# Rows of the modulation product in buffers of their own beside the branch merge, and another order of the first norm

## Chip, cores, metric

The kernel runs on one core of a Trainium2 chip. The metric is the device time of one execution in microseconds. Three runs are shown, and their median counts.

## What is computed

The reference is one layer of a diffusion backbone over 512 latent tokens of width 1024 and 256 context tokens. Cut to the parts that the change touches:

```python
mx = (sil_c @ w_ada[l] + b_ada[l])[:, None, :]          # modulation: 6 vectors of 1024
xsh1, xsc1, xg1, xsh2, xsc2, xg2 = jnp.split(mx, N_ADA, axis=-1)
px = _split_in(_modulate(x, xsh1, xsc1) @ w_in[l])
...
mix_x = _merge(px['merge_gate'], hgrn_out, conv_out, ox_att @ w_att_o[l], w_out[l])
x = _layer_norm(ALPHA * x + xg1 * mix_x, ln1_g[l], ln1_b[l])
x = _layer_norm(ALPHA * x + xg2 * _peer(_modulate(x, xsh2, xsc2), peer_wq[l], ...), ...)
```

`_merge` is the sum over three branches of sigmoid(gate) times the branch's output product, then a product with `w_out`. `_peer` makes queries (16 products with `wq`), picks the 16 best experts of each head and token, and evaluates gelu of tokens times all rows of `peer_u` (128 products here, called u products) for three of the four token blocks, with gathers for block 0.

## The kernel before

Data lie transposed, features on the 128 partitions. A float32 product is done in three passes (`mm3`): each operand is split into a high part (rounded copy, ScalarE, `whi`) and a low part (difference, VectorE or GpSimd, `wlo`), and TensorE adds low*high, high*low and high*high. A weight of 128 output columns is 512 KB; `wload` fetches it on SP's queue into one of 3 buffers `wraw`, splits it in two halves into 8 buffers each of `whi` and `wlo` (four weights), and a product over it is 24 matmuls. The orders of TensorE, VectorE, ScalarE and GpSimd are written out by hand: what stands in the code first is issued first. SP's order is left to the framework.

Weights come through a list: `want` appends, `fetch_next(n)` loads and splits the next one if fewer than n (3) stand ready, `feed` hands over the next one and fetches it on the spot if none is ready. `go` takes one step of a generator, `run` all of it.

**The merge.** After the 8 products of the HGRN branch (`hg`, evacuated by the multiply in line 749) a loop over 8 column blocks does two products each: the gate (`'in', Z_MG + KT + j`; sigmoid in line 781 into `s`) and the convolution branch (`'conv', j`; multiply in line 788, then GpSimd's add in line 789). Each loop turn also does four of the 32 rows of the modulation vectors that are needed later (`adas`): a row of `w_adaT` (512 KB) times silu(c), summed over the free axis by one VectorE instruction (line 763, shown as CUSTOM_DVE). The rows pass through the same list and the same 3 `wraw` buffers as the weights:

```python
for n, w in ((0, ('in', Z_MG + KT + j)), (2, ('conv', j)), (3, None)):
    want(*[('ada', a) for a in steps[:n] if a is not None])
...
if w[0] == 'ada':
    raw = wp.tile([128, KT, 128], F32, name="wraw", bufs=3)
    nc.sync.dma_start(raw, src)
```

So each turn has six items in a list that is at most three ahead, with four calls of `fetch_next`. The attention follows the merge; its first products wait for the last multiply of the merge, since the PSUM pool changes there.

**Norm 1.** After attention and the output projection (`project(h_, b)`, half h_ of block b, blocks in the order 1, 2, 3, 0) each block gets its residual and statistics on VectorE (`project`, `moments1`), the scale by a power on GpSimd (`pspow`, line 154) and a GpSimd multiply (line 1149), the normalisation on ScalarE (`normalise`, line 1154), transposes on TensorE (`turn1`), modulation out of PSUM (`modulate`, half on VectorE in line 1177, half on ScalarE in line 1175) and the split into `thl` (`parts1`). The u product 0 needs blocks 1 to 3 and fills the time while block 0 is finished (tile `pu`); the first query product needs all blocks. After that the expert search (top-k) runs on VectorE beside the query and u products.

Of the kernel before, what the change touches and what calls it, by code (L numbers as in the profile page):

```python
# [94 lines left out]
def body(tc, I, O):  # L95
# [139 lines left out]
    TABLE = {'hg': 'w_hg_o', 'conv': 'w_conv_o', 'att': 'w_att_o'}  # L235
    LOWS = {'in': (V, G), 'hg': (V, G), 'conv': (V, G), 'att': (V, V)}

    def source(kind, *i):
        if kind == 'ada':
            return I['w_adaT'][i[0]].rearrange("p (k e) -> p k e", e=128), None  # L240
        if kind == 'u':
            return I['uT'][i[0]].rearrange("p (k e) -> p k e", e=128), (V, G)
        return I[TABLE.get(kind, 'w_in')][i[0]], LOWS[kind]

# [17 lines left out]
    def fetch_next(n=3):  # L262

        if todo and len(ready) < n:
            w = todo.pop(0)
            src, subs = source(*w)
            if w[0] == 'ada':
                raw = wp.tile([128, KT, 128], F32, name="wraw", bufs=3)
                nc.sync.dma_start(raw, src)
                ready.append((w, raw))  # L270
                return
            ready.append((w, wload(None, subs, loaded.pop(0)) if loaded else wload(src, subs)))
# [17 lines left out]
    want(*[('hg', j) for j in range(KT)])  # L290
    steps = [a for j in range(32) for a in ((j,) if j % 4 < 3 else (j, None))]
    for j in range(KT):
        for n, w in ((0, ('in', Z_MG + KT + j)), (2, ('conv', j)), (3, None)):
            want(*[('ada', a) for a in steps[:n] if a is not None])
            del steps[:n]
            want(*([w] if w else []))
    want(*[('in', z) for z in (Z_AK, Z_AQ, Z_AV, Z_AQ + 1)])
# [461 lines left out]
    def adas():  # L759

        for j in range(32):
            raw = feed('ada', j)[:].rearrange("p k e -> p (k e)")
            V.tensor_tensor_reduce(out=raw, in0=raw, in1=silb, scale=1.0, scalar=0.0, op0=ALU.mult, op1=ALU.add,
                                   accum_out=mod[:, 16 + j, 0:1])
            yield
            if j % 4 == 3:
                m = mod[:, 13 + j:17 + j, 0]
                V.tensor_add(m, m, bada[:, 13 + j:17 + j])
                yield
# [80 lines left out]
    want(*[('in', Z_MG + 16 + j) for j in range(KT)])  # L850
    want(*[('att', j) for j in range(KT)], ('u', 0))

# [250 lines left out]
    pus = ExitStack()  # L1103
    pu = pus.enter_context(tc.tile_pool(name="pu", bufs=1, space=PSUM))
    ops = ExitStack()
# [24 lines left out]
    def project(h_, b):  # L1130
# [5 lines left out]
        sl = slice(h_ * 512, h_ * 512 + 512)  # L1136
        V.tensor_mul(t_, ps, g1[:, sl])
        V.scalar_tensor_tensor(x1[:, b, sl], x1[:, b, sl], ALPHA, t_, op0=ALU.mult, op1=ALU.add)
        V.bn_stats(bst[b][:, h_, :], x1[:, b, sl])
# [3 lines left out]
    def moments1(b):  # L1143
# [4 lines left out]
        pspow(rs[:, 0:1], mv[:, 1:2], 1.0, mv[:, 1:2])  # L1148
        G.tensor_mul(rs[:, 1:2], rs[:, 0:1], mv[:, 0:1])

    def normalise(b):
        xb = x1[:, b, :]
        rs = moms[b]
        A.activation(xb, xb, AF.Identity, scale=rs[:, 0:1], bias=rs[:, 1:2])
        nc.scalar.dma_start(x1d[b], xb)

# [11 lines left out]
    def modulate(b, pts):  # L1168
        tfs = []
        for q_, pt in enumerate(pts):  # L1170
            tf = op.tile([128, 4, 128], F32, name="tf", bufs=4)
            for i in range(4):
                j = q_ * 4 + i
                if q_ or b == 3:
                    A.activation(tf[:, i, :], pt[:, i, :], AF.Identity, scale=gs[:, j:j + 1], bias=bs[:, j:j + 1])
# [5 lines left out]
    def parts1(b, tfs):  # L1181
        for q_, tf in enumerate(tfs):
            sl = (slice(None), slice(q_ * 4, q_ * 4 + 4), slice(b * 128, b * 128 + 128))
            split(thl[0][sl], thl[1][sl], tf)

# [8 lines left out]
    for i, b in enumerate(BLOCKS):  # L1194
        wout(4 + i)
        project(0, b)
    thl = [xp.tile([128, KT, T], F32R, name=n) for n in ("xh", "xl")]
    for i, b in enumerate(BLOCKS[:3]):
        project(1, b)
        if i:  # L1200
# [7 lines left out]
        fetch_next(4)  # L1208
    project(1, 0)
    pts = turn1(3)  # L1210
    moments1(0)
    tfs = modulate(3, pts)
    fetch_next(4)
    parts1(3, tfs)
    normalise(0)
    for _ in range(3):
# [3 lines left out]
    ttok = x1p.tile([128, D], F32, name="ttok")  # L1220
    us = pu.tile([128, T], F32, name="pu")[:, :T - 128]
    p_ = product(us, feed('u', 0), [t_[:, :, 128:] for t_ in thl], 4)
    go(p_)
    pts = turn1(0)
    go(p_)
    tfs = modulate(0, pts)
    parts1(0, tfs)
    UV = {}
    UV['q', 0] = wload(I['wq'][0], (V, G))
    fetch_next(4)  # L1230
    turn_back(tfs)
# [23 lines left out]
    arun = gap.tile([128, NA, TD], F32, name="gt")  # L1255
    A.activation(arun[:, 0, :], us, AF.Gelu_apprx_tanh)
    pus.close()
# [39 lines left out]
    for h in range(H):  # L1297
        u0 = 1 + sum(AHEAD[:h])
        items += [('q', 2 * h), ('q', 2 * h + 1)] + [('u', u0 + i) for i in range(AHEAD[h])]
    items += [('u', i) for i in range(1 + sum(AHEAD), NU)]  # L1300
    SUBS = {'q': (G, G), 'u': (G, G)}
# [493 lines left out]
```

## Time and profile before

| | |
|---|---|
| median of 3 runs | 2467.76 us (2458.68 to 2470.45) |
| the profiled execution | 2469.7 us, span 2467.8 us |
| TensorE busy | 2356.6 us (95%), granted clock 0.986 of full speed on average |
| VectorE busy | 1937.8 us (79%) |
| ScalarE, GpSimd busy | 1044.3 us (42%), 667.5 us (27%) |
| DMA | 452.66 MB, mean 183 GB/s |

The span is the stretch between the first and the last instruction in the trace; times below are microseconds from its start. Busy shares are means over stages with different limits, so each stage is read by itself. Matmuls are pipelined, so a busy TensorE is not one at its peak.

### The profile page before, as it was taken

How to read it: one execution, taken by the hardware profiler on the slowest of the kernel's cores; microseconds unless marked ns; L12 is line 12 of the kernel's file. 1: busy time of each engine (PE TensorE's matmuls, PEld its weight loads, DVE VectorE, ACT ScalarE, POOL GpSimd, SP SyncE). 2: the span in 40 equal slices, each digit the busy share in tenths (PEclk: the TensorE clock that was granted, in tenths of full speed). 3: DMA queues.
4: the chain of work that ended last, by engine and by line, in shares of the span. 5: the costliest groups of instructions: out<-in, count | busy, mean ns of one | idle time of the engine just before them, and what ended most of it. 6: DMA issues, size and time to landing. Idle time of an engine off the chain costs nothing.

```text
span 2467.8 us, 34756 instructions
## 1 busy us (share of the span) xinstructions
PE 2356.6 (95%) x12547; PEld 2028.7 (82%) x12547; DVE 1937.8 (79%) x3722; ACT 1044.3 (42%) x2298; POOL 667.5 (27%) x564
## 2 busy tenths in 40 slices
PE   7999999999988999999999999999999999999997
PEld 3888888887767777787899999987777889898886
DVE  7788888887665566564899789968878888889886
ACT  5544444434312444643457655533333333333333
POOL 6000000003122000031688401122323344444432
PEclk9999999999999999999999999999999999999999
DMA  6211111112364111132333368999999989999962
GB/s 243 69 60 61 61 60 60 52 65 72 134 212 158 43 35 35 52 111 103 105 112 103 121 241 308 330 321 317 335 368 348 350 317 344 324 336 320 331 223 96
DMA packets 156973, 452.66 MB, mean 183 GB/s; under 512 B 16256, under 2 KB 60672, under 8 KB 154624
## 3 DMA queue, kind: packets, MB, share of 16 engines
q1 hardware_dynamic: 106976, 278.33, 32.7%
q0 software_dynamic: 36864, 134.23, 15.3%
q10 hardware_dynamic: 12960, 37.87, 4.1%
q8 instruction: 99, 1.62, 0.3%
q14 instruction: 74, 0.61, 0.1%
HBM read 411.77 MB, written 37.03 MB: 182 GB/s over the span
## 4 chain that ended last, share of the span: by engine, by line
PE 57%; DVE 25%; DMA 6%; ACT 5%; issue 4%; POOL 2%; ACTq 0%; DVEq 0%; SPq 0%; POOLq 0%
PE mm L142 13%; PE mm L144 12%; PE mm L143 12%; DVE wlo L131 6%; DVE raw L1488 3%; DVE ttok L1496 3%; DMA wraw<-in_v_dram 3%; ACT whi L129 2%; PE sc L466 2%; PE pg L1538 2%; ACT ph L137 2%; DMA wraw<-in_uT_dram 2%; PE acc L142 1%; PE acc L143 1%; PE acc L144 1%
## 5 line engine op out<-in xcount | busy, mean ns | idle before, releaser
L131 DVE TENSOR_TENSOR wlo<-wraw,whi 128x512 fp32r<-128x512 f32 x680 | 453.1, 708 | 186.1 <-ACT whi L129 184.2
L142 PE MATMUL mm<-xh,wlo 128*128 128x512 f32 (+1 forms) x1456 | 559.7, 384 | 17.8 <-DVE wlo L131 5.5
L143 PE MATMUL mm<-xl,whi 128*128 128x512 f32 (+1 forms) x1456 | 540.3, 371 | 1.1 <-POOL xl L327 0.9
L144 PE MATMUL mm<-xh,whi 128*128 128x512 f32 (+1 forms) x1456 | 540.5, 371 | 0.0
L129 ACT ACTIVATE whi<-wraw 128x512 fp32r<-128x512 f32 x784 | 447.5, 621 | 121.3 <-DMA wraw<-in_w_in_dram 46.2
L142 PE MATMUL acc<-whi,pl 128*128 128x512 f32 x756 | 300.4, 397 | 23.9 <-DVE pl L138 18.8
L142 PEld LDWEIGHTS mm<-xh,wlo 128*128 128x128 f32 x1456 | 275.8, 189 | 53.1 <-DVE wlo L131 6.8
L144 PEld LDWEIGHTS mm<-xh,whi 128*128 128x128 f32 x1456 | 275.0, 189 | 37.2
L143 PEld LDWEIGHTS mm<-xl,whi 128*128 128x128 f32 x1456 | 275.8, 189 | 34.0 <-DVE xl L327 1.8
L143 PE MATMUL acc<-wlo,ph 128*128 128x512 f32 x756 | 301.5, 399 | 2.1 <-DVE wlo L131 0.9
L144 PE MATMUL acc<-whi,ph 128*128 128x512 f32 x756 | 298.6, 395 | 0.0
L1477 POOL DMA_INDIRECT raw<-in_u_dram,idx x128 | 147.4, 1151 | 472.1 <-DVE act L1488 413.5
L1477 POOL DMA_INDIRECT raw<-in_v_dram,idx x128 | 160.5, 1254 | 193.0 <-DVE ttok L1496 156.1
L142 PEld LDWEIGHTS acc<-whi,pl 128*128 128x128 f32 x756 | 143.8, 190 | 62.4 <-ACT whi L129 16.7
L137 ACT ACTIVATE ph<-a 128x384 fp32r<-128x384 f32 x94 | 49.4, 525 | 332.5 <-DVE a L1601 323.3
L561 DVE SCALAR_TENSOR_TENSOR u<-up,dw,u 128x512 f32<-128x512 f32 x240 | 179.6, 748 | 4.9
L131 POOL TENSOR_TENSOR wlo<-wraw,whi 128x512 fp32r<-128x512 f32 x104 | 149.2, 1457 | 123.0 <-ACT whi L129 116.6
L143 PEld LDWEIGHTS acc<-wlo,ph 128*128 128x128 f32 x756 | 143.7, 190 | 42.7 <-DVE wlo L131 13.4
L144 PEld LDWEIGHTS acc<-whi,ph 128*128 128x128 f32 x756 | 143.6, 190 | 28.5
L1496 DVE SCALAR_TENSOR_TENSOR ttok<-raw,act,ttok 128x1024 f32<-128x1024 f32 x127 | 162.9, 1283 | 3.1
L142 PE MATMUL pa<-xh,wlo 128*128 128x384 f32 x456 | 154.7, 339 | 6.4 <-DVE wlo L131 6.4
L144 PE MATMUL pa<-xh,whi 128*128 128x384 f32 x456 | 154.5, 339 | 0.0
(422 smaller groups left out, 4255.6 us busy)
## 6 DMA issues: line engine op xcount, KB each, us to landing
wraw<-in_uT_dram SPq DMA_DIRECT2D x128, 512.0 KB, 5.0
wraw<-in_v_dram SPq DMA_DIRECT2D x128, 512.0 KB, 6.2
wraw<-in_w_in_dram SPq DMA_DIRECT2D x96, 512.0 KB, 3.3
gd<-gs ACTq DMA_DIRECT2D x16, 1536.0 KB, 7.5
gr<-gd SPq DMA_DIRECT2D x60, 288.0 KB, 9.1
wraw<-in_w_adaT_dram SPq DMA_DIRECT2D x32, 512.0 KB, 4.4
wraw<-in_wq_dram SPq DMA_DIRECT2D x16, 512.0 KB, 3.3
ad<-a ACTq DMA_DIRECT2D x39, 192.0 KB, 4.2
```

The lines of the kernel that those rows point to most:

```text
L129: A.activation(hi, r, AF.Copy)
L131: subs[i].tensor_sub(lo, r, hi.bitcast(F32))
L137: A.activation(hi, src, AF.Copy)
L142: P.matmul(out, ll, rh, start=first, stop=False)
L143: P.matmul(out, lh, rl, start=False, stop=False)
L144: P.matmul(out, lh, rh, start=False, stop=last)
L466: P.matmul(x_.ps[:, b, :], x_.KM[:, b * 128:(b + 1) * 128], ap3(x_.QP, T + b * 128, [2 * w_, 64 // w_], [w_ - T, 2], [1, w_]), start=True, ...
L561: V.scalar_tensor_tensor(acc, up[:, i:i + T], dw[:, j, i:i + 1], acc, op0=ALU.mult, op1=ALU.add)
L1477: G.indirect_dma_start(out=r, out_offset=None, in_=I['u'] if n < NS_ else I['v'], in_offset=bass.IndirectOffsetOnAxis(ap=idx0[:, n % NS_:n ...
L1488: V.tensor_tensor_reduce(out=r, in0=r, in1=ttok, scale=1.0, scalar=0.0, op0=ALU.mult, op1=ALU.add, accum_out=act[:, s_:s_ + 1])
L1496: V.scalar_tensor_tensor(ysb, r, act[:, s_:s_ + 1], ysb, op0=ALU.mult, op1=ALU.add)
L1538: P.matmul(ps[:, i, :], o3[:, q_, :, i], o1[:, i, :], start=q_ == 0, stop=q_ == 1)
```

## The change

The rows of `w_adaT` leave the list. They get a tile of their own of four rows, in the place of the tile `ohi` (the high part of the HGRN output, free after the last `hg` product), loaded three rows ahead of the reduction. The low parts of the conv weights are made on VectorE alone. In norm 1, the last projection (block 0) only evacuates PSUM before block 3 is modulated and split; its residual and statistics come behind that. The multiply behind the power moves from GpSimd to VectorE, the write of the normalised block to DRAM moves behind the split, block 0 is normalised in two halves, VectorE takes five of eight modulations of block 3, and GpSimd makes the low parts of block 2. Two u products instead of one are computed ahead of the queries (`PRE = 2`), so the later u products are one fewer; the gelu of both stands before the queries' evacuation.

```diff
-    LOWS = {'in': (V, G), 'hg': (V, G), 'conv': (V, G), 'att': (V, V)}
+    LOWS = {'in': (V, G), 'hg': (V, G), 'conv': (V, V), 'att': (V, V)}
...
-            if w[0] == 'ada':
-                raw = wp.tile([128, KT, 128], F32, name="wraw", bufs=3)
-                nc.sync.dma_start(raw, src)
-                ready.append((w, raw))
-                return
...
-    steps = [a for j in range(32) for a in ((j,) if j % 4 < 3 else (j, None))]
     for j in range(KT):
-        for n, w in ((0, ('in', Z_MG + KT + j)), (2, ('conv', j)), (3, None)):
-            want(*[('ada', a) for a in steps[:n] if a is not None])
-            del steps[:n]
-            want(*([w] if w else []))
+        want(('in', Z_MG + KT + j), ('conv', j))
...
     def adas():
-        for j in range(32):
-            raw = feed('ada', j)[:].rearrange("p k e -> p (k e)")
+        raws = mp.tile([128, 4, D], F32, name="ohi")
+        for j in range(-3, 32):
+            if j + 3 < 32:
+                nc.sync.dma_start(raws[:, (j + 3) % 4, :], I['w_adaT'][j + 3])
+            if j < 0:
+                continue
+            raw = raws[:, j % 4, :]
             V.tensor_tensor_reduce(out=raw, in0=raw, in1=silb, scale=1.0, scalar=0.0, op0=ALU.mult, op1=ALU.add,
                                    accum_out=mod[:, 16 + j, 0:1])
...
-    pu = pus.enter_context(tc.tile_pool(name="pu", bufs=1, space=PSUM))
+    PRE = 2
+    pu = pus.enter_context(tc.tile_pool(name="pu", bufs=PRE, space=PSUM))
...
         V.tensor_mul(t_, ps, g1[:, sl])
+        yield
         V.scalar_tensor_tensor(x1[:, b, sl], x1[:, b, sl], ALPHA, t_, op0=ALU.mult, op1=ALU.add)
...
-        G.tensor_mul(rs[:, 1:2], rs[:, 0:1], mv[:, 0:1])
+        V.tensor_mul(rs[:, 1:2], rs[:, 0:1], mv[:, 0:1])
...
-        A.activation(xb, xb, AF.Identity, scale=rs[:, 0:1], bias=rs[:, 1:2])
-        nc.scalar.dma_start(x1d[b], xb)
+        for xb in ([x1[:, b, :]] if b else [x1[:, b, :512], x1[:, b, 512:]]):
+            A.activation(xb, xb, AF.Identity, scale=rs[:, 0:1], bias=rs[:, 1:2])
...
-                if q_ or b == 3:
+                if j > 4 if b == 3 else q_:
...
-            split(thl[0][sl], thl[1][sl], tf)
+            A.activation(thl[0][sl], tf, AF.Copy)
+            (G if b == 2 else V).tensor_sub(thl[1][sl], tf, thl[0][sl].bitcast(F32))
+        nc.scalar.dma_start(x1d[b], x1[:, b, :])
...
-    project(1, 0)
+    last = project(1, 0)
+    go(last)
     pts = turn1(3)
-    moments1(0)
     tfs = modulate(3, pts)
     fetch_next(4)
     parts1(3, tfs)
+    run(last)
+    moments1(0)
     normalise(0)
...
-    us = pu.tile([128, T], F32, name="pu")[:, :T - 128]
-    p_ = product(us, feed('u', 0), [t_[:, :, 128:] for t_ in thl], 4)
+    us = [pu.tile([128, T], F32, name="pu")[:, :T - 128] for _ in range(PRE)]
+    p_ = chain([product(us[i], feed('u', i), [t_[:, :, 128:] for t_ in thl], 4) for i in range(PRE)])
+    go(p_)
+    fetch_next(4)
     go(p_)
     pts = turn1(0)
-    go(p_)
     tfs = modulate(0, pts)
-    parts1(0, tfs)
     UV = {}
     UV['q', 0] = wload(I['wq'][0], (V, G))
-    fetch_next(4)
+    parts1(0, tfs)
+    run(p_)
     turn_back(tfs)
```

Three places show how the instructions move. First ScalarE in the merge, between two sigmoids of gate products (`mm_6038` is the product of gate j = 1; the weight split from `wraw_6072` is the conv weight of j = 1, the product right behind that gate, and `wraw_6113` is the gate weight of j = 2, the next one). Before:

```order
L781 ACTIVATE ms_6069<-mm_6038 128x512
L129 ACTIVATE whi_6074<-wraw_6072 128x512
L129 ACTIVATE whi_6078<-wraw_6072 128x512
L129 ACTIVATE whi_6115<-wraw_6113 128x512
L129 ACTIVATE whi_6119<-wraw_6113 128x512
L781 ACTIVATE ms_6156<-mm_6125 128x512
```

The same place of the change (`mm_6058` is again gate j = 1; `wraw_6114` and `wraw_6154` are the gate and conv weights of j = 3, four and five products further on):

```order
L775 ACTIVATE ms_6097<-mm_6058 128x512
L129 ACTIVATE whi_6116<-wraw_6114 128x512
L129 ACTIVATE whi_6120<-wraw_6114 128x512
L129 ACTIVATE whi_6156<-wraw_6154 128x512
L129 ACTIVATE whi_6160<-wraw_6154 128x512
L775 ACTIVATE ms_6180<-mm_6141 128x512
```

The splits behind a sigmoid are now those of weights that TensorE reads one pair of products or more later, not of the next product.

Second, SP's queue in the merge before (`in_w_in` are gate weights, `in_w_conv_o` conv weights, `in_w_adaT` modulation rows):

```order
L124 DMA wraw<-in_w_conv_o_dram 128x1024
L269 DMA wraw<-in_w_adaT_dram 128x1024 x2
L124 DMA wraw<-in_w_in_dram 128x1024
L269 DMA wraw<-in_w_adaT_dram 128x1024 x2
L124 DMA wraw<-in_w_conv_o_dram 128x1024
```

and of the change, from the first load of a modulation row on:

```order
L124 DMA wraw<-in_w_conv_o_dram 128x1024
L753 DMA ohi<-in_w_adaT_dram 128x1024 x8
L124 DMA wraw<-in_w_in_dram 128x1024
L753 DMA ohi<-in_w_adaT_dram 128x1024 x3
L124 DMA wraw<-in_w_conv_o_dram 128x1024
L753 DMA ohi<-in_w_adaT_dram 128x1024
L124 DMA wraw<-in_w_in_dram 128x1024
```

Before, rows and weights take turns in one ring of three buffers. Now six weights of the merge stand ahead of the first row, and rows go to another tile.

Third, VectorE at the end of norm 1 before (`tf<-pt` is a modulation, `xl<-tf` the low part, `t<-mm` the evacuation of the last projection, BN_STATS and BN_AGGR its statistics):

```order
L1137 TENSOR_TENSOR t<-mm,g_9579 128x512
L1138 SCALAR_TENSOR_TENSOR x_9571<-x_9571,t 128x512
L1139 BN_STATS bst_9608<-x_9571 128x6
L1145 BN_AGGR bmv<-bst_9608 128x2
L1146 TENSOR_SCALAR bmv<-bmv 128x1
L153 TENSOR_SCALAR bmv<-bmv 128x1
L138 TENSOR_TENSOR xl<-tf,xh 128x4x128 x2
L1177 TENSOR_SCALAR tf<-pt,gs,bs 128x128 x4
L138 TENSOR_TENSOR xl<-tf,xh 128x4x128 x2
L131 TENSOR_TENSOR wlo<-wraw,whi 128x512 x2
```

and in the change:

```order
L1132 TENSOR_TENSOR t<-mm,g_9558 128x512
L1172 TENSOR_SCALAR tf<-pt,gs,bs 128x128 x5
L1180 TENSOR_TENSOR xl<-tf,xh 128x4x128 x2
L1134 SCALAR_TENSOR_TENSOR x_9550<-x_9550,t 128x512
L1135 BN_STATS bst_9587<-x_9550 128x6
L1141 BN_AGGR bmv<-bst_9587 128x2
L1142 TENSOR_SCALAR bmv<-bmv 128x1
L153 TENSOR_SCALAR bmv<-bmv 128x1
L1145 TENSOR_TENSOR brs<-brs,bmv 128x1
L1172 TENSOR_SCALAR tf<-pt,gs,bs 128x128 x4
L131 TENSOR_TENSOR wlo<-wraw,whi 128x512
L1180 TENSOR_TENSOR xl<-tf,xh 128x4x128 x2
```

Block 3 now comes ahead of the statistics of block 0, and the first query weight's low part ahead of the low parts of block 0. On TensorE the 8 transposes of block 0 stood behind 12 matmuls of the u product; they now stand behind 36.

## Rows read from the trace of the kernel before

**Rows 1.** The page: shares of the last-ending chain, and the low-part group's row.

```profile
PE 57%; DVE 25%; DMA 6%; ACT 5%; issue 4%; POOL 2%; ACTq 0%; DVEq 0%; SPq 0%; POOLq 0%
L131 DVE TENSOR_TENSOR wlo<-wraw,whi 128x512 fp32r<-128x512 f32 x680 | 453.1, 708 | 186.1 <-ACT whi L129 184.2
```

**Rows 2.** Windows in the merge: length, five engines' busy time, clock, DMA share, GB/s.

```profile
655.00:770.00 115.00, 97.08 (x383) 75.20 (x381) 72.47 (x105) 21.24 (x38) 30.87 (x14) 0.94 0.63 213
660.00:670.00 10.00, 10.00 (x44) 7.86 (x43) 6.92 (x11) 1.75 (x3) 2.21 (x1) 1.00 0.82 274
770.00:780.00 10.00, 8.62 (x36) 7.14 (x37) 4.05 (x8) 3.37 (x6) 1.29 (x1) 0.83 0.58 194
```

**Rows 3.** Timeline of VectorE before and in the merge (start, us, instruction, idle before).

```profile
649.10 0.69 DVE L749 TENSOR_TENSOR mix<-mm,mix 128x512 f32<-128x512 f32 x1 [3.54 <-PE mm L144]
654.70 0.69 DVE L749 TENSOR_TENSOR mix<-mm,mix 128x512 f32<-128x512 f32 x1 [4.91 <-PE mm L144]
666.15 0.68 DVE L788 TENSOR_TENSOR ms<-mm,ms 128x512 f32<-128x512 f32 x1
...
681.43 1.21 DVE L763 CUSTOM_DVE_ANT_0 wraw<-wraw,silb 128x1024 f32<-128x1024 f32 x1
...
682.57 2.31 DVE L763 CUSTOM_DVE_ANT_0 wraw<-wraw,silb 128x1024 f32<-128x1024 f32 x1
...
770.65 0.68 DVE L788 TENSOR_TENSOR ms<-mm,ms 128x512 f32<-128x512 f32 x1
```

**Rows 4.** Timelines of ScalarE and TensorE: one turn of the merge, and its end.

```profile
701.18 0.60 ACT L781 ACTIVATE ms<-mm 128x512 f32<-128x512 f32 x1 [6.10 <-PE mm L144]
701.67 1.14 ACT L129 ACTIVATE whi<-wraw 128x512 fp32r<-128x512 f32 x2
708.88 1.15 ACT L129 ACTIVATE whi<-wraw 128x512 fp32r<-128x512 f32 x2 [6.07 <-DMA wraw<-in_w_in_dram]
...
703.07 0.50 PE L142 MATMUL mm<-uhi,wlo 128*128 128x512 f32 x1 [1.99 <-DVE wlo L131]
...
771.38 0.50 PE L142 MATMUL mm<-xh,wlo 128*128 128x512 f32 x1 [2.75 <-DVE ms L788]
```

**Rows 5.** The tile wraw from 655 to 770: its 47 loads, issue to landing.

```profile
DMA to landing us min/median/max: 3.1/4.3/5.5
```

**Rows 6.** Timelines of TensorE, ScalarE and VectorE at norm 1.

```profile
1167.01 0.44 PE L142 MATMUL pu<-xh,wlo 128*128 128x384 f32 x1 [3.34 <-ACT xh L137]
...
1170.66 1.73 PE L1164 MATMUL pt<-ident,x 128*128 128x128 f32 x8
...
1172.58 0.33 PE L144 MATMUL pu<-xh,whi 128*128 128x384 f32 x1
...
1174.14 0.34 PE L144 MATMUL pu<-xh,whi 128*128 128x384 f32 x1
...
1176.44 0.50 PE L142 MATMUL mm<-xh,wlo 128*128 128x512 f32 x1 [1.09 <-DVE wlo L131]
...
1163.55 2.88 ACT L1175 ACTIVATE tf<-pt,bs,gs 128x128 f32<-128x128 f32 x8
...
1168.39 1.24 ACT L1154 ACTIVATE x<-x,brs 128x1024 f32<-128x1024 f32 x1 [0.92 <-POOL brs L1149]
...
1173.82 1.16 ACT L137 ACTIVATE xh<-tf 128x512 fp32r<-128x512 f32 x2
...
1159.76 1.36 DVE L1177 TENSOR_SCALAR tf<-pt,gs,bs 128x128 f32<-128x128 f32 x4
...
1188.63 0.89 DVE L1372 MAX8 vv<-sk 128x8 f32<-128x128 f32 x4 [3.55 <-PE sk L1331]
```

**Rows 7.** Windows of the later stages: top-k, gate products, gathers (columns as above).

```profile
1260.00:1280.00 20.00, 20.00 (x106) 18.09 (x105) 19.90 (x97) 12.51 (x65) 17.11 (x18) 1.00 0.35 111
...
1520.00:1540.00 20.00, 20.00 (x165) 19.21 (x164) 19.83 (x29) 11.28 (x16) 2.29 (x2) 1.00 0.94 332
...
1760.00:1800.00 40.00, 37.41 (x159) 29.28 (x158) 31.06 (x56) 14.32 (x27) 10.71 (x10) 1.00 1.01 376
```

More of the change, by code (lines that the diff above doesn't have):

```diff
@@ L235, in body @@
     TABLE = {'hg': 'w_hg_o', 'conv': 'w_conv_o', 'att': 'w_att_o'}
-    LOWS = {'in': (V, G), 'hg': (V, G), 'conv': (V, G), 'att': (V, V)}
+    LOWS = {'in': (V, G), 'hg': (V, G), 'conv': (V, V), 'att': (V, V)}
     def source(kind, *i):
-        if kind == 'ada':
-            return I['w_adaT'][i[0]].rearrange("p (k e) -> p k e", e=128), None
         if kind == 'u':
@@ L850, in body @@
     want(*[('in', Z_MG + 16 + j) for j in range(KT)])
-    want(*[('att', j) for j in range(KT)], ('u', 0))
+    want(*[('att', j) for j in range(KT)], ('u', 0), ('u', 1))
     kTs, Vas = {}, {}
@@ L1148, in moments1 @@
         pspow(rs[:, 0:1], mv[:, 1:2], 1.0, mv[:, 1:2])
-        G.tensor_mul(rs[:, 1:2], rs[:, 0:1], mv[:, 0:1])
+        V.tensor_mul(rs[:, 1:2], rs[:, 0:1], mv[:, 0:1])
     def normalise(b):
-        xb = x1[:, b, :]
         rs = moms[b]
-        A.activation(xb, xb, AF.Identity, scale=rs[:, 0:1], bias=rs[:, 1:2])
-        nc.scalar.dma_start(x1d[b], xb)
+        for xb in ([x1[:, b, :]] if b else [x1[:, b, :512], x1[:, b, 512:]]):
+            A.activation(xb, xb, AF.Identity, scale=rs[:, 0:1], bias=rs[:, 1:2])
     def turn1(b):
@@ L1195, in body @@
         wout(4 + i)
-        project(0, b)
+        run(project(0, b))
     thl = [xp.tile([128, KT, T], F32R, name=n) for n in ("xh", "xl")]
     for i, b in enumerate(BLOCKS[:3]):
-        project(1, b)
+        run(project(1, b))
         if i:
@@ L1255, in body @@
     arun = gap.tile([128, NA, TD], F32, name="gt")
-    A.activation(arun[:, 0, :], us, AF.Gelu_apprx_tanh)
+    for i in range(PRE):
+        A.activation(arun[:, i, :], us[i], AF.Gelu_apprx_tanh)
     pus.close()
@@ L1297, in body @@
     for h in range(H):
-        u0 = 1 + sum(AHEAD[:h])
+        u0 = PRE + sum(AHEAD[:h])
         items += [('q', 2 * h), ('q', 2 * h + 1)] + [('u', u0 + i) for i in range(AHEAD[h])]
-    items += [('u', i) for i in range(1 + sum(AHEAD), NU)]
+    items += [('u', i) for i in range(PRE + sum(AHEAD), NU)]
     SUBS = {'q': (G, G), 'u': (G, G)}
```

## Prediction

> **What bounds the kernel now.** First I read the chain that ended last on the page: TensorE holds 57% of it, VectorE 25%, DMA 6%, ScalarE 5% [rows 1]. So the kernel is paced mostly by TensorE, and what counts are the places where TensorE stands still. The low-part group names one: VectorE made 680 low parts and sat 184.2 us ahead of them waiting for ScalarE's high parts [rows 1]. That says that splits come late, not that VectorE is short of time.
>
> Then I read the windows, to find the stage. In the merge, 655 to 770, TensorE is busy 97.08 of 115 us at a granted clock of 0.94, while VectorE has 72.47, ScalarE 21.24, GpSimd 30.87, and the transfers run at 213 GB/s with a share of 0.63 [rows 2]. Nothing is full there, and yet TensorE waits. How much it loses is seen on the instructions that evacuate its products. Two evacuations in the `hg` loop are 5.60 us apart (649.10 and 654.70): that is one product of 24 matmuls at TensorE's own pace. In the merge the conv evacuations should be two products apart, 11.20 us. The first is at 666.15, which is still on pace (654.70 + 11.20 = 665.90), the last at 770.65: seven turns in 104.50 us, 14.93 us each [rows 3].
>
> The timelines of one turn show why. ScalarE ends the wait for a gate product with the sigmoid (701.18), and only then, at 701.67, splits the conv weight that TensorE needs next, so TensorE starts the conv product at 703.07 after standing 1.99 us. ScalarE's next split, of the gate weight, waited 6.07 us for its transfer, which had waited for a buffer that a modulation row held [rows 4]. Each item is split just before it is used: the list holds six items a turn and is three ahead. At the end the first attention product starts at 771.38, after a further wait of 2.75 us for the last multiply [rows 4], and the stretch 770 to 780 has a granted clock of 0.83: behind the standstill TensorE runs a part of it at the lower of its two levels [rows 2].
>
> **The change part by part: the merge.** The rows leave the list, so a turn has two weights for four fetches, and the weights run ahead to the limit of three; the order shows splits of weights that are read a pair of products or more later. TensorE then no longer waits for a split, if four things hold.
>
> *Transfers.* From 654.7 on, 32 rows, ten merge weights and three attention weights have to land, 45 loads of 0.524 MB or 23.6 MB, in 16 x 5.60 = 89.6 us: 263 GB/s. The stage reached 274 GB/s in 660 to 670, at a share of 0.82 [rows 2], and a later stage held 376 over 40 us [rows 7]. So it fits, without much to spare if 274 were the limit (86 us for the bytes) and with plenty if 376 is (63 us). The Trainium skill, on its page "DMA: Bandwidth & Descriptors", section Specifications, gives about 358 GB/s as what HBM yields per core; an estimate from that figure is 66 us for these bytes, which is on the side of the later row. That row lies a little above the page's figure, and the measurement decides.
>
> *The rows' own latency.* The first row can only be requested when the last `hg` product has read `ohi`, about 654.6, one product before its use; a load lands in 4.3 us (3.1 to 5.5) [rows 5]. VectorE will stand some 3 us at the first reduction and perhaps a little at the next three. Behind it in VectorE's queue are the low parts of the weight for the fifth product, which TensorE reads at 654.7 + 4 x 5.60 = 677; even 10 us late they are in time. After that each row is requested four reductions ahead, some 10 us, twice the landing time. On SP's queue a weight may stand behind three rows that wait for reductions; with weights two products (11 us) ahead this costs nothing. If the cover fails, a late split costs what it does now, about 2 us each.
>
> *VectorE.* A turn needs four reductions (1.21 us), four low parts (0.708 us on average), the multiply (0.68 us) and once the 1.1 us by which a reduction grows when GpSimd adds at the same time (2.31 against 1.21 us) [rows 1, 3]: 4.84 + 2.83 + 0.68 + 1.1 = 9.45 us of 11.20. The low part of conv that moves from GpSimd to VectorE is in it; it fits.
>
> *ScalarE* has four splits and a sigmoid, under 3 us [rows 4].
>
> So the seven slow turns shrink by 14.93 - 11.20 = 3.73 us each: **-26.1 us**. Then the clock: the wait of 2.75 us before attention becomes about 1 us (evacuation and multiply, since no splits stand ahead of it). After the change TensorE has no long standstill before attention, so the low stretch goes: (1 - 0.83) x 10 = **-1.7 us**. The wait itself is already counted: the last evacuation moves with the turns. Bounds: nothing gained if transfers stay at 213 GB/s (23.6 MB then take 111 us, 654.7 + 111 = 765.7, gain 5); at most 27.8 + 1 by the shorter wait.
>
> **Norm 1.** What starts u product 0 is the split of block 3. Before, ScalarE did its eight modulations in 2.88 us from 1163.55, and u product 0 began at 1167.01 after 3.34 us of standstill [rows 6]. Now VectorE first evacuates the last projection (0.69), then does five modulations at 0.34 (four take 1.36 [rows 6]), and ScalarE three at 0.36, which write the tile that VectorE's fifth writes and so may come after it: 0.69 + 1.7 + 1.08 = 3.5 us against 2.88, from a start about 0.5 us earlier. I take no change; 1.1 us earlier if the two engines overlap.
>
> Behind that, the statistics of block 0 stand after five modulations and two low parts, 3 us later, so its normalisation starts about 1171.3 instead of 1168.39 [rows 6]. That is hidden, because TensorE now does 36 u matmuls before block 0's transposes instead of 12. These 24 cost 9 x 0.173 us per nine (1172.58 to 1174.14 [rows 6]), 24 x 0.173 = 4.15 us. The transposes therefore end at 1172.39 + 4.15 = 1176.5. From there to the first query product it took 4.05 us before (1176.44). Now modulation 1.44 + 0.1, the first query weight's split, put ahead on ScalarE, 1.15, the first copy 0.6 and its low part 0.65: 3.9 us. The queries start at about 1180.4, **+4.0 us**. The second half of u product 1 and the turn-back lie under this.
>
> VectorE's top-k is full (19.90 of 20 [rows 7]) and starts from the first scores, so this delay goes through it. What comes back is the u product that is no longer to be done. Where gate products run, TensorE is busy 20.00 of 20 us and VectorE 19.83 [rows 7]: there TensorE, by a little, sets the pace, and one u product less is **-4.15 us**. Net -0.15. Bounds: +4.0 if VectorE sets the pace there, and +1.2 on top if top-k's constants come late (they wait for the last DRAM write of block 0, which moves behind its split; VectorE had 3.55 us idle before the first maximum [rows 6]); -4 if top-k absorbs the delay. The multiply on VectorE instead of GpSimd replaces one instruction in a chain of small ones, and VectorE waits there some 0.9 us for the power, as ScalarE did [rows 6], in time in which it would wait for TensorE anyway: nothing. The low parts of block 2 on GpSimd, which has no other work there, are done while block 3 is modulated: nothing. The extra split of u weight 1 falls into the attention output, where GpSimd and ScalarE have room: nothing.
>
> **Sum.** -26.1 - 1.7 - 0.15 = -28 us. The profiled execution took 2469.7 us, so it would take 2441.7; it is 1.9 us above the median of the runs shown, so the median goes to **2440 us**. Everything behind the merge is tied to TensorE or to transfers that begin later by the same amount, so an earlier start is kept to the end.
>
> **The rivals.**
>
> *Transfers as the new limit* (chance 0.13). Rows and weights together need 263 GB/s, and the three weight buffers and four row buffers cannot keep that up. For it: the stage's best 10 us had 274. Against it: 376 later with the same size of load. At 235 GB/s the merge takes 100 us instead of 89.6, the gain is 17, and the time 2451.
>
> *The change doesn't do what it says* (0.06). The weights still arrive just in time, because SP serves its queue in order and a weight stands behind rows that wait for reductions. At today's 213 GB/s the gain is 5, the time 2463.
>
> *Rows one by one* (0.05), the slower side. If a row's load and the reductions in the same tile exclude one another, each of 32 reductions waits for a load that was issued only after the one before: 0.33 issue + 4.3 landing + 1.21 = 5.85 us. VectorE's low parts are queued behind them, so the merge takes 32 x 5.85 = 187 us, 97 longer than 89.6 and 70 longer than now: 2538. It decides once a reduction costs over 116.7 / 32 = 3.65 us in all. Against it: the four rows are separate ranges, and each load waits for one reduction only.
>
> *The forecast* (0.76) is the rest: the merge at TensorE's pace, norm 1 between -4 and +5.
>
> **How the numbers follow.** A measurement of this kernel tells about 0.5%, 12.3 us, from no change; its three runs lie 11.8 us apart. The forecast's own range is 2430 to 2447. To hold 8 in 10 I go to the transfer rival's middle and a bit beyond: 2430 to 2456. Faster than 2455.4 are the forecast and most of the transfer rival: 0.87. Within 0.5%: 0.08, the rest of it and today's pace. Slower: 0.05.
>
> **What would show it.** Right: conv evacuations 11.2 us apart, no wait of about 2 us before conv products, the first attention product near 745, a granted clock near 1.00 in the ten us behind it, and transfers around 260 GB/s in the merge. In norm 1: a standstill of about 3 us before u product 0 as now, queries starting 13 us after it instead of 9.4, and the gate products ending about 28 us earlier than now. Wrong: reductions that wait for their rows throughout (the transfer or one-by-one rival); SP waiting with a weight behind rows; or a merge on pace whose gain shrinks before the gathers, which would mean that VectorE or the transfers of the last stage, not TensorE, set its end.

## The result and the profile after

The changed kernel took **2431.94 us** (median of four runs, 2430.52 to 2440.56) where the kernel before took 2463.73 beside it (four runs): a ratio of 0.9876, interval 0.9845 to 0.9907. The profiled execution is the longest of the four, 2440.56 us with a span of 2438.8, so traces are compared with traces: 2467.8 to 2438.8 is -29.0 us.

The page's chain and its low-part group, which answer to [rows 1]:

```profile
PE 60%; DVE 24%; DMA 7%; ACT 5%; issue 3%; POOL 2%; ACTq 0%; DVEq 0%; POOLq 0%; SPq 0%
L131 DVE TENSOR_TENSOR wlo<-wraw,whi 128x512 fp32r<-128x512 f32 x687 | 465.1, 719 | 156.3 <-ACT whi L129 155.0
```

VectorE waits 29 us less for ScalarE's high parts (155.0 against 184.2 us). The windows of the merge and of the ten us behind it (columns as in [rows 2]):

```profile
655.00:744.00 89.00, 88.06 (x382) 71.31 (x381) 70.17 (x113) 22.41 (x39) 12.49 (x8) 1.00 0.80 282
660.00:670.00 10.00, 10.00 (x45) 8.12 (x44) 9.13 (x15) 1.82 (x4) 1.67 (x1) 1.00 0.77 265
744.00:754.00 10.00, 10.00 (x64) 8.96 (x62) 1.43 (x3) 2.96 (x6) 0.11 (x1) 1.00 0.20 59
```

TensorE is now busy 88.06 of 89 us at full clock, the transfers run at 282 GB/s instead of 213, and VectorE has 19 us left. VectorE's timeline, which answers to [rows 3] (L738 evacuates `hg`, L757 is the reduction, L782 the conv evacuation):

```profile
653.35 0.69 DVE L738 TENSOR_TENSOR mix<-mm,mix 128x512 f32<-128x512 f32 x1 [3.71 <-PE mm L144]
...
657.35 1.23 DVE L757 CUSTOM_DVE_ANT_0 ohi<-ohi,silb 128x1024 f32<-128x1024 f32 x1 [0.90 <-DMA ohi<-in_w_adaT_dram]
...
660.84 1.23 DVE L757 CUSTOM_DVE_ANT_0 ohi<-ohi,silb 128x1024 f32<-128x1024 f32 x1 [1.11 <-DMA ohi<-in_w_adaT_dram]
...
664.53 0.68 DVE L782 TENSOR_TENSOR ms<-mm,ms 128x512 f32<-128x512 f32 x1
...
742.06 0.69 DVE L782 TENSOR_TENSOR ms<-mm,ms 128x512 f32<-128x512 f32 x1 [1.82 <-PE mm L144]
```

Seven turns (passes of the merge loop) take 742.06 - 664.53 = 77.53 us, **11.08 us each**. The last evacuation waits 1.82 us for TensorE; TensorE waits once, 0.94 us for that evacuation, before attention. The view of the rows' tile says how much of their latency is seen:

```profile
its engine sat idle before it (us, times) until:
  DMA ohi<-in_w_adaT_dram: 2.0, 2
...
DMA to landing us min/median/max: 4.1/5.4/7.4
```

Two of 32 reductions waited, 2.0 us in all, though a row now takes 5.4 us to land, where the 47 loads of before took 4.3 [rows 5]. One turn on ScalarE and the start of attention on TensorE, which answer to [rows 4]:

```profile
703.20 0.60 ACT L775 ACTIVATE ms<-mm 128x512 f32<-128x512 f32 x1 [4.91 <-PE mm L144]
703.70 1.14 ACT L129 ACTIVATE whi<-wraw 128x512 fp32r<-128x512 f32 x2
...
742.89 0.47 PE L142 MATMUL mm<-xh,wlo 128*128 128x512 f32 x1 [0.94 <-DVE ms L782]
```

The split behind the sigmoid is still there, but it is that of a later weight, and TensorE waits for no split between 653.35 and 742.89. Norm 1, which answers to [rows 6] (L1159 transposes, L1179 and L1180 high and low parts, L1170 and L1172 modulations on ScalarE and VectorE, L1150 normalisation):

```profile
1136.85 0.69 PE L142 MATMUL pu<-xh,wlo 128*128 128x384 f32 x1 [3.21 <-ACT xh L1179]
...
1146.17 1.03 PE L1159 MATMUL pt<-ident,x 128*128 128x128 f32 x8
...
1150.36 0.49 PE L142 MATMUL mm<-xh,wlo 128*128 128x512 f32 x1 [0.17 <-ACT xh L1179]
1151.74 0.50 PE L143 MATMUL mm<-xl,whi 128*128 128x512 f32 x1 [0.89 <-DVE xl L1180]
...
1135.13 1.16 ACT L1170 ACTIVATE tf<-pt,bs,gs 128x128 f32<-128x128 f32 x3 [2.56 <-DVE tf L1172]
...
1140.87 1.52 ACT L1150 ACTIVATE x<-x,brs 128x512 f32<-128x512 f32 x2 [3.55 <-DVE brs L1145]
...
1163.71 0.89 DVE L1373 MAX8 vv<-sk 128x8 f32<-128x128 f32 x4 [3.28 <-PE sk L1332]
```

U product 0 starts 30.2 us earlier than before, the queries only 26.1, the first maximum of top-k only 24.9: norm 1 costs 4.1 us at the queries and 5.2 at top-k. The last gate product starts at 1589.8 instead of 1618.1: -28.3, so 3.4 us of that come back while TensorE has one u product less to do.

| milestone | before | after | difference |
|---|---|---|---|
| last `hg` evacuation | 654.70 | 653.35 | -1.35 |
| first attention product | 771.38 | 742.89 | -28.49 |
| first matmuls waiting for the squares in attention (`ars`) | 787.48 | 757.31 | -30.17 |
| u product 0 | 1167.01 | 1136.85 | -30.16 |
| first query product | 1176.44 | 1150.36 | -26.1 |
| first maximum | 1188.63 | 1163.71 | -24.9 |
| last gate product | 1618.1 | 1589.8 | -28.3 |
| end | 2467.8 | 2438.8 | -29.0 |

### The profile page after: what moved, and what is told of

It reads as the page before. It is cut to its first block, busy times and chain, and to the rows that moved or that the text cites. A ratio compares the mean times of both kernels' runs of the same rounds, so it can differ in the third digit from the quotient of the medians.

```text
span 2438.8 us, 34766 instructions
## 1 busy us (share of the span) xinstructions
PE 2344.7 (96%) x12547; PEld 2022.8 (83%) x12547; DVE 1935.6 (79%) x3736; ACT 1043.3 (43%) x2294; POOL 648.6 (27%) x555
## 4 chain that ended last, share of the span: by engine, by line
PE 60%; DVE 24%; DMA 7%; ACT 5%; issue 3%; POOL 2%; ACTq 0%; DVEq 0%; POOLq 0%; SPq 0%
PE mm L142 13%; PE mm L144 13%; PE mm L143 13%; DVE wlo L131 6%; DVE raw L1489 4%; DMA wraw<-in_v_dram 3%; PE sc L455 2%; PE pg L1539 2%; ACT whi L129 2%; PE acc L142 2%; PE acc L143 2%; PE acc L144 2%; ACT ph L137 2%; DMA wraw<-in_uT_dram 2%; DVE ttok L1497 2%
## 5 line engine op out<-in xcount | busy, mean ns | idle before, releaser
L131 DVE TENSOR_TENSOR wlo<-wraw,whi 128x512 fp32r<-128x512 f32 x687 | 465.1, 719 | 156.3 <-ACT whi L129 155.0
L142 PE MATMUL mm<-xh,wlo 128*128 128x512 f32 (+1 forms) x1448 | 555.9, 384 | 12.4 <-POOL wlo L131 3.8
L131 POOL TENSOR_TENSOR wlo<-wraw,whi 128x512 fp32r<-128x512 f32 x97 | 132.8, 1391 | 89.3 <-ACT whi L129 87.3
```

Source lines behind the costliest of these rows:

```text
L131: subs[i].tensor_sub(lo, r, hi.bitcast(F32))
L142: P.matmul(out, ll, rh, start=first, stop=False)
```

## The experiments

Ratios are to the kernel before beside each run; "turn" is the mean of the seven distances between conv evacuations. Kernels whose turns take 11.08 or 11.09 us have medians from 2431.9 to 2441.0, so smaller differences between medians are not read as effects.

| kernel | turn, us | median, us | ratio and interval |
|---|---|---|---|
| before | 14.93 | 2463.7 | 1 |
| after | 11.08 | 2431.9 | 0.9876 (0.9845 to 0.9907) |
| merge_only | 11.09 | 2434.2 | 0.9868 (0.9852 to 0.9883) |
| norm_only | 14.94 | 2467.0 | 1.0002 (0.9987 to 1.0017) |
| list_own | 13.76 | 2457.4 | 0.9960 (0.9944 to 0.9976) |
| refill_own | 11.32 | 2438.0 | 0.9894 (0.9875 to 0.9913) |
| out_shared | 14.74 | 2468.6 | 1.0014 (1.0002 to 1.0026) |
| refill_shared | 19.79 | 2506.0 | 1.0161 (1.0144 to 1.0178) |
| slots1 | 19.38 | 2511.5 | one run |
| slots2 | 12.66 | 2453.0 | 0.9953 (0.9936 to 0.9969) |
| slots3 | 11.09 | 2441.0 | 0.9896 (0.9879 to 0.9912) |
| rows_twice | 15.54 | 2472.0 | 1.0021 (1.0008 to 1.0035) |
| conv_g | 11.09 | 2437.2 | 0.9886 (0.9869 to 0.9902) |
| trans24 | 11.09 | 2438.0 | 0.9878 (0.9858 to 0.9897) |

### Each half of the change alone

**merge_only** is the kernel before with the pieces of the diff up to `adas`, norm 1 untouched.

> Only the merge part of the change: rows out of the list, in their own four-row tile, conv low parts on VectorE; norm 1 as before. By my theory the merge alone gives 27 us of turns and 1.7 us of clock behind it, so about 2436 us, ratio 0.988; first attention product near 743 us, u product 0 about 30 us earlier than before, and the lead of 30 us kept to the end. Rival (the gain of the whole change came in good part from norm 1): the ratio stays above 0.993.

Measured 2434.2 us, 0.9868: the merge alone gives the whole gain.

**norm_only** is the kernel before with the other pieces alone (from `PRE = 2` on).

> Only the norm 1 part; merge as before. By my theory the queries start 4 us later and the gate products end at about the same time as before (+4.0 - 4.15, from the change's trace +5.2 - 3.3 at most), so 2464 us, ratio 0.999 to 1.001. Rival (the delay of top-k is lost and the u product gives nothing): +4 us, ratio 1.002. Rival (norm 1 gives a part of the gain): below 0.997.

Measured 1.0002 (0.9987 to 1.0017, or -3 to +4 us): nothing that can be told. Its timeline shows both halves of the zero, on TensorE and VectorE:

```profile
1167.13 0.44 PE L142 MATMUL pu<-xh,wlo 128*128 128x384 f32 x1 [3.21 <-ACT xh L1185]
...
1179.86 0.50 PE L142 MATMUL mm<-xh,wlo 128*128 128x512 f32 x1 [0.17 <-ACT xh L1185]
...
1193.16 0.89 DVE L1379 MAX8 vv<-sk 128x8 f32<-128x128 f32 x4 [2.12 <-PE sk L1338]
```

The queries start 12.7 us behind u product 0 instead of 9.4, the first maximum is 4.5 us later than before; the last gate product starts at 1619.2 instead of 1618.1, 1.1 us later. The third theory (a part of the gain) is out; between the first two the time cannot tell, but the trace gives 3.4 us back.

### The list or the buffers

Two things could have made the merge slow: rows and weights share three buffers, and rows stand between the weights in one list. Four kernels part them.

**list_own**: the kernel before, rows in the list as before, in buffers of their own. The added condition only holds the rows back until their tile exists.

```diff
-        if todo and len(ready) < n:
+        if todo and len(ready) < n and (todo[0][0] != 'ada' or arows):
...
-                raw = wp.tile([128, KT, 128], F32, name="wraw", bufs=3)
-                nc.sync.dma_start(raw, src)
+                raw = arows[0][:, w[1] % 4, :]
+                nc.sync.dma_start(raw, I['w_adaT'][w[1]])
...
+    arows.append(mp.tile([128, 4, D], F32, name="ohi"))
     a_ = adas()
```

> Kernel before with one thing changed: the rows stay in the list, in the same places and three ahead, but have four buffers of their own (the tile ohi). Theory A (the place in the list makes splits late): the conv weight is still split behind the sigmoid, TensorE still stands about 2 us before each conv product, so turns of about 13.2 us and a gain of 12 to 14 us. Theory B (three buffers shared with the rows limit the transfers, 213 GB/s): with seven buffers the turns reach 11.2 us and the gain is 26 us or more.

Measured 2457.4 us. TensorE still waits for the split before each conv product:

```profile
689.04 0.69 PE L142 MATMUL mm<-uhi,wlo 128*128 128x512 f32 x1 [1.99 <-DVE wlo L131]
703.90 0.50 PE L142 MATMUL mm<-uhi,wlo 128*128 128x512 f32 x1 [1.99 <-DVE wlo L131]
```

That is a gain of 8 us (6 to 14 by the interval), a little under theory A's 12 to 14. Five turns took 13.3 us, as theory A has it, the other two 14.9. The extra 1.6 us are not another wait. The windows behind these two standstills of the same length (the third number from the right is the granted clock):

```profile
689.00:693.00 4.00, 3.96 (x10) 3.12 (x11) 3.97 (x6) 0.82 (x2) 2.26 (x1) 0.57 0.19 57
704.00:708.00 4.00, 4.00 (x18) 3.23 (x19) 3.96 (x7) 0.68 (x2) 2.14 (x1) 1.00 0.21 59
```

After the first, TensorE ran over 3 us at the lower of its two levels and did 10 matmuls where it did 18 after the second. Theory B is out as the only cause, and what own buffers give without a fuller list is a third of the gain.

**out_shared**: the kernel after, rows out of the list, but in the three buffers of the weights.

```diff
-        raws = mp.tile([128, 4, D], F32, name="ohi")
-        for j in range(-3, 32):
...
+        rows = []
+        for j in range(-1, 32):
+            if j + 1 < 32:
+                raw = wp.tile([128, KT, 128], F32, name="wraw", bufs=3)
+                nc.sync.dma_start(raw, I['w_adaT'][j + 1].rearrange("p (k e) -> p k e", e=128))
+                rows.append(raw)
```

> Kernel after with one thing changed: the rows are out of the list, requested one reduction ahead, but use the three buffers wraw that the weights use. Theory A (the place in the list): weights are three products ahead, splits are early, and most of the gain stays, turns of 11.2 to 12 us. Theory B (buffers limit the transfers): at 213 GB/s the 23.6 MB still take 111 us, turns of about 14 us, and the gain in the merge falls from 27 to about 5 us. If VectorE waits for each row behind the ring it could be worse than before.

Measured 1.0014: the gain is gone, as theory B has it. The window and, from the view of the tile `wraw` over the same 80 us, who waited:

```profile
660.00:740.00 80.00, 73.17 (x308) 58.37 (x307) 42.72 (x75) 15.10 (x27) 6.46 (x5) 0.98 0.65 216
```

```profile
  DMA wraw<-in_w_in_dram: 42.9, 6
...
  DMA wraw<-in_w_conv_o_dram: 21.4, 5
  DMA wraw<-in_w_adaT_dram: 11.1, 6
```

216 GB/s, about the rate of before. In 80 us ScalarE waits 64 us for weights, and VectorE, whose low parts and multiplies stand behind those splits and rows, is late for TensorE, which waits 16.6 us for the last multiply. This kernel differs from after in two things, for it also requests its rows one reduction ahead instead of three. slots2 (below) has that depth in buffers of its own, and its turns take 12.66 us. Of the 3.66 us by which the turns here are longer than in after, 1.58 thus go with the depth and 2.08 with the sharing. So neither alone is enough: own buffers without a full list leave the wait before the conv products, and weights ahead of the rows without own buffers wait for their transfers.

**refill_own**: list_own with one line. It came from counting the list: a turn takes six items and fills four times, so the list runs empty and the conv weight is fetched on the spot.

```diff
             raw = feed('ada', j)
+            fetch_next()
```

> As list_own (rows in the list, four buffers of their own), with one line more: behind each row that is taken from the list, the list is filled up again. Before, a turn takes six items and fills four times, so the list is empty when the conv weight is due, and that weight is fetched on the spot. If the empty list is what made splits late: no wait before conv products, turns of 11.1 to 11.3 us, about 2435 us. Rival (the rows' places between the weights delay them even in a full list): turns stay at 12.5 us or more, above 2445 us.

Measured 2438.0 us. Its window, and TensorE's only wait in it:

```profile
660.00:740.00 80.00, 79.72 (x346) 64.51 (x345) 69.14 (x96) 19.37 (x37) 27.29 (x14) 1.00 0.81 290
```

```profile
661.57 0.50 PE L142 MATMUL mm<-uhi,wlo 128*128 128x512 f32 x1 [0.28 <-DVE wlo L131]
```

Six turns of 11.08 to 11.15 us (the last had 12.72): the rows may stand in the list, if it is kept full. The second low part of each conv weight is still made by GpSimd here, so moving it to VectorE is not what gives the gain.

**refill_shared**: the same line in the kernel before.

> The kernel before with that one line: the list is filled up behind each row, rows and weights still share three buffers. Theory (both limits are real, and the ring of three allows 210 GB/s): turns of 14 to 15 us as before, 2455 to 2470 us, TensorE waiting less at the conv products but VectorE and the transfers late. Rival (the empty list alone was the cause): turns of 11 to 12 us, about 2440 us.

Measured 1.0161, 41 us **slower** than before, which neither theory had. From its window and from the waits of SP's queue (waited for: us in total, times, longest):

```profile
660.00:740.00 80.00, 60.34 (x223) 45.70 (x221) 34.48 (x54) 11.84 (x21) 10.29 (x8) 0.89 0.53 177
```

```profile
SPq L269 <- DVE wlo L131: 30.8, 8, 6.2
SPq L269 <- DMA wraw<-in_w_in_dram: 18.3, 4, 4.6
```

Fetching further ahead into the same three buffers makes them turn more slowly: loads of rows now wait up to 6.2 us for a weight's low part. In these 80 us no reduction waits for its row, while ScalarE waits 67.3 us for weights: rows that have landed keep their buffers until VectorE reaches them, and weights come late. The rate falls to 177 GB/s. A deeper list is worth something only with buffers for its depth.

### How many rows in flight, and how much the transfers can give

**slots1**, **slots2** and **slots3** are the kernel after with fewer slots (here two):

```diff
-        for j in range(-3, 32):
-            if j + 3 < 32:
-                nc.sync.dma_start(raws[:, (j + 3) % 4, :], I['w_adaT'][j + 3])
+        for j in range(-1, 32):
+            if j + 1 < 32:
+                nc.sync.dma_start(raws[:, (j + 1) % 2, :], I['w_adaT'][j + 1])
...
-            raw = raws[:, j % 4, :]
+            raw = raws[:, j % 2, :]
```

> Kernel after, but the tile of rows has one slot instead of four: each row is requested only when the one before has been reduced. Theory (a row's latency then lies on VectorE's path): 0.33 issue + 3.1 to 4.3 landing + 1.21 reduction = 4.6 to 5.85 us for each of 32 rows, so the merge takes 149 to 187 us instead of 89.5, the time is 2491 to 2530 us and VectorE waits for a transfer at nearly every reduction. Rival (SP or the other work hides it): under 2450 us.

> Kernel after, but two slots instead of four. Theory: two rows per 5.85 us or somewhat more (landing took 5.4 us with four in flight), so four rows take 11.7 to 14 us where a turn of TensorE has 11.08: turns of 11.7 to 14 us, 4 to 20 us slower than after (2436 to 2452 us). Rival (two slots hide the latency as well as four): 2432 us and turns of 11.08 us.

> Kernel after with three slots for rows instead of four. One slot took 155.7 / 32 = 4.9 us a row, two took 12.66 / 4 = 3.2 us a row, which is 6.3 us per row and slot. With three slots at 6.3 to 7 us: 2.1 to 2.3 us a row, 8.4 to 9.3 us for four, under TensorE's 11.08: on pace, 2432 us. Rival (a row's time grows in step with the slots, so that two slots' rate is a limit of the transfers): turns above 12 us, 2445 us or more.

With one slot the merge (from the last `hg` to the last conv evacuation) took 155.7 us, 4.9 us a row, and VectorE waited for every row (the tile's view, us and times):

```profile
  DMA ohi<-in_w_adaT_dram: 81.3, 32
```

With two slots the turns took 12.66 us; the median is 21 us above that of after, and in the trace attention starts 15 us later (1.8 of them from `hg`) and the end comes 10.8 us later. TensorE does not show it from 660 to 740, where it was busy 79.94 of 80 us; it paid at the end, in one wait:

```profile
757.95 0.77 PE L142 MATMUL mm<-xh,wlo 128*128 128x512 f32 x1 [13.87 <-DVE ms L782]
```

Three slots are on pace, 11.09. The median of 2441.0 us is 9 us above the 2432 expected, but the intervals of the two ratios overlap, and in the traces the end differs by 3.3 us, 2.0 of them from `hg`. So the slots are a latency matter: 4.9, 3.2 and under 2.8 us a row.

**rows_twice** fetches a second row beside each into the tile `olo`, which nobody reads.

```diff
+        more = mp.tile([128, 4, D], F32, name="olo")
...
+                nc.sync.dma_start(more[:, (j + 3) % 4, :], I['w_adaT'][31 - j - 3])
```

> Kernel after, and beside each row a second row is fetched into another tile of four slots that nobody reads: 77 loads or 40.4 MB in the merge instead of 45 or 23.6. It asks where transfers would become the limit. If the limit is the 376 GB/s of the later stage: 107 us instead of 89.5, about 2450 us. If it is the 290 GB/s that the merge now moves: 139 us, about 2482 us. If the transfers have still more room: no change, 2432 us, which 450 GB/s would need.

The merge took 122.0 us for 40.4 MB, 331 GB/s over all and 355 in its middle, and ScalarE waited for weights:

```profile
660.00:740.00 80.00, 68.23 (x271) 53.84 (x271) 43.81 (x73) 13.74 (x25) 6.83 (x5) 0.92 0.94 355
```

```profile
L129 ACT ACTIVATE whi<-wraw 128x512 fp32r<-128x512 f32 x20 | 11.6, 625 | 58.3 <-DMA wraw<-in_w_in_dram 43.6 <-DMA wraw<-in_w_conv_o_dram 11.4 <-PE mm L144 3.3
```

So the 282 GB/s of after leave room: 1.17 to 1.26 times that rate was moved here. The expectation from 376 GB/s (107 us) was too kind, that from 290 (139 us) too strict. The Trainium skill, "DMA: Bandwidth & Descriptors", section Specifications, gives about 358 GB/s from HBM per core; the 355 here lie just under that figure and the 376 of [rows 7] above it, so these runs do not show it as a ceiling.

### Small parts

**conv_g** sets `'conv': (V, G)` in the kernel after.

> Kernel after, but the second low part of each conv weight on GpSimd again, as before. By my theory that part of the change is worth nothing: TensorE sets the pace with weights far ahead and VectorE has time left in a turn: 2432 us, ratio to after within 0.2%. Rival (GpSimd's slower low part or its port shared with VectorE delays the reductions): VectorE's waits grow and turns get longer than 11.08 us, 2436 us or more.

Turns of 11.09 us and 0.9886 (0.9869 to 0.9902): the move of that low part is worth nothing that can be told. Its median is 5 us above that of after, beyond the 0.2% expected and past the 2436 of the rival, but the turns did not get longer, the intervals overlap, and its trace ends at 2438.4 against 2438.8.

**trans24** moves block 0's transposes behind 24 u matmuls.

```diff
-    p_ = chain([product(us[i], feed('u', i), [t_[:, :, 128:] for t_ in thl], 4) for i in range(PRE)])
-    go(p_)
+    ps_ = [product(us[i], feed('u', i), [t_[:, :, 128:] for t_ in thl], 4) for i in range(PRE)]
+    go(ps_[0])
     fetch_next(4)
-    go(p_)
+    run(ps_[0])
     pts = turn1(0)
+    p_ = ps_[1]
```

> Kernel after, with block 0's transposes behind 24 instead of 36 matmuls of the u products. Theory: what delays the queries is the second u product itself, 24 matmuls that TensorE has to do before them; moving the transposes only takes out the wait of about 1 us around them: queries 12.4 us behind the start of u product 0 instead of 13.5, time the same within 0.1%. Rival (block 0's chain of modulation and splits behind the transposes sets the queries): 3 us earlier queries, and 3 us off the time.

```profile
1137.41 0.69 PE L142 MATMUL pu<-xh,wlo 128*128 128x384 f32 x1 [3.21 <-ACT xh L1179]
...
1150.45 0.47 PE L142 MATMUL mm<-xh,wlo 128*128 128x512 f32 x1
...
1162.60 0.90 DVE L1374 MAX8 vv<-sk 128x8 f32<-128x128 f32 x4 [2.74 <-PE sk L1333]
```

The queries start 13.0 us behind u product 0 (13.5 in after, 12.4 expected), now without the wait of 0.89 us for the low part, and the first maximum comes 25.2 us behind it instead of 26.9. TensorE's own 24 matmuls remain: the rival of 3 us is out. The time is that of after within what can be told, so none of these kernels is shown to beat it.

## Why the prediction was right, step by step

*The sum.* Predicted -28.0 for the profiled execution (2441.7 us); it took 2440.6. In the traces the parts are -27.1 for the merge, -1.7 for the clock, +1.9 for norm 1 and -1.35 that belong to no part of the change, together -28.3 at the last gate product, and -0.7 behind it. That the sum came so close is in part luck: the 1.35 us and the 1.0 us more in the merge make up for the 2 us that norm 1 missed. The medians differ by 31.8 us, interval 23 to 38. The forecast of 2440 lies 8 us above the measured 2431.9: its base, the median of three runs, was 2.5 us above the 2465.3 of the 23 runs beside merge_only, and the rest lies within the interval.

*The merge, -26.1.* Measured -27.1 from the last `hg` evacuation to the first attention product. The turns reached 11.08, not 11.20 us, since a pair of merge products is a little shorter than two of `hg`; seven times 0.12 is most of the difference. All four conditions held. Transfers reached 282 GB/s where 263 were needed, but had less room in rows_twice than the later stage's row promised. The rows' own latency cost 2.0 us instead of 3 and was hidden. VectorE was busy 70.17 of 89 us, a smaller share than the 9.45 of 11.20 worked out, and the 1.1 us by which it slows beside GpSimd's add falls on low parts now (two in 2.38 us at 665.13, in 1.29 elsewhere), not on a reduction. ScalarE was busy 22.41 of 89 us.

*Why the turns were slow.* Here one step was incomplete and one was misread. The prediction put a late split down to a list that "holds six items a turn and is three ahead". Three ahead is only the limit: with four fills for six items the list runs empty, and refill_own shows that keeping it full is enough, given buffers.

The misread step is that the gate weight's transfer "had waited for a buffer that a modulation row held". The rows named for it show the wait for the transfer, not the buffer. The trace shows another holder: GpSimd ended the low part of the conv weight at 702.94 + 2.35 = 705.29, and the load of the gate weight went out at 705.32.

```profile
702.94 2.35 POOL L131 TENSOR_TENSOR wlo<-wraw,whi 128x512 fp32r<-128x512 f32 x1 [4.17 <-ACT whi L129]
...
705.32 0.33 SPq L124 DMA_DIRECT2D wraw<-in_w_in_dram  x1
```

From 660 to 740 the loads of weights (L124) waited mostly for low parts and those of rows (L269) mostly for reductions:

```profile
SPq L124 <- DVE wlo L131: 23.6, 10, 3.0
SPq L269 <- DVE mod L763: 18.4, 12, 2.2
SPq L124 <- POOL wlo L131: 10.2, 5, 2.3
```

So a weight was loaded only when the low part of another weight was done, and in the turn shown that was the weight right before it. The rows took buffers from the weights all the same, which is why buffers of their own help; but it was a weight, not a row, that held the one waited for.

The clock is the other part. A slow turn lost 3.85 us of which the wait of 1.99 us is little more than half. TensorE's matmuls of before by line from 655 to 770, those with the first operand of a conv and of a gate product (busy, mean ns, idle before them):

```profile
L142 PE MATMUL mm<-uhi,wlo 128*128 128x512 f32 x64 | 28.5, 446 | 13.9 <-DVE wlo L131 13.9
...
L142 PE MATMUL mm<-xh,wlo 128*128 128x512 f32 x63 | 25.0, 397 | 2.7 <-DVE wlo L131 2.7
```

That is 16.6 us of waits. At a mean clock of 0.94 [rows 2] TensorE lost, by an estimate from that mean, 115 x 0.06 = 6.9 us more behind them (conv matmuls take 446 ns on average, gate matmuls 397), and the last wait became 1.8 us shorter: 25.3 of the 27.1. The rest is about what list_own's turns of 13.3 us hold beside their wait, 0.25 us each. The size was right because it was taken from evacuations, which hold it all.

*The clock, -1.7.* The stretch behind the merge runs at 1.00, and attention gained 1.68 us between its first product and the `ars` matmuls.

*Norm 1, -0.15.* U product 0 stands still 3.21 us (3.34 before); queries +4.1 (forecast +4.0). Two sizes were off: top-k starts 5.2 us later, not 4.0, because the second query matmul waits 0.89 us for block 0's low part (trans24, without that wait, has only 3.6 on the same measure), and the u product gives back 3.4, not 4.15. From u product 0 to the last gate product that is +1.9 us; norm_only has +1.0 and no difference in time. The constants of top-k came in time.

*The rivals.* Transfers as the limit: not here, but real at one and a quarter times the rate (rows_twice). Rows one by one: not in the change, and slots1, which makes it so, costs 4.9 us a row where the rival had 5.85, and 2511 us where it had 2538. The change doing nothing because weights stand behind rows on SP: no, weights are early enough.

*What is not the change.* 1.35 us of the -29.0 arise before the merge, in `hg`. Both traces have the same standstills of 1.35 and 0.88 us at 606 us; the window behind them, before and then after:

```profile
608.00:612.00 4.00, 3.73 (x10) 2.94 (x11) 4.00 (x8) 3.52 (x7) 0.41 (x1) 0.61 0.38 131
```

```profile
608.00:612.00 4.00, 3.52 (x15) 2.89 (x16) 4.00 (x8) 3.73 (x8) 0.19 (x1) 1.00 0.42 131
```

The lower clock follows them in 7 of the 14 traces here, among them kernels with and without the change.

## What to carry to other kernels

A queue of prefetches needs two things together: as many fills as takes, and a buffer for each item of its depth. Here neither more buffers nor an earlier order was worth more than a third of the gain alone, and more depth without buffers made it 1.6% slower. Read the loss of a slow loop from the distance of its evacuations, not from its waits, since the clock behind a wait can cost nearly as much as the wait (1.6 us behind one of 1.99 in list_own). When a load waits for a buffer, look up which instruction ended just before the load went out, instead of guessing who held it. Work that is only moved ahead of a full engine, as the second u product was, comes back as work that is not done later, and the sum is near nothing.

## What was not expected of the hardware

The same standstill, of 1.99 us in list_own and of 1.35 and 0.88 us in `hg`, was followed by some 3 us at the lower clock level in some places and by none in others. What decides between them stays open. The Trainium skill, "TensorE: Matmul & The Clock Gate", section "HAM oscillation — how this bites in real kernels", describes a loop that waits for transfers in each turn and begins each next piece at the lower level. The merge of before agrees with it in part: TensorE stands still in each turn, though for a split, and the mean clock is 0.94 over 115 us, but only four of the seven waits before conv products were followed by a fall (clock 0.57 to 0.67 in the 4 us behind them; 1.00 behind the other three).

The landing time rose from 4.3 us (rows and weights of before) to 5.4 us (rows of after) while the rate rose from 213 to 282 GB/s, and it did not matter, since the slots covered it.
